# Level exponents of gated linear attention: from one running sum by subtraction on DVE, in place of eight mask products on TensorE

## The chip, the core and the metric

The kernel runs on one core of a Trainium2 chip. The metric is the device time of one execution in microseconds (us); lower is better. Instructions run on TensorE (PE; its weight loads are listed as PEld), VectorE (DVE), ScalarE (ACT) and GpSimd (POOL). SyncE (SP) issues DMA transfers and does no arithmetic. Each engine executes its own list of instructions in a fixed order. Where an instruction needs what another engine has not yet made, it waits, and everything behind it on its engine waits with it.

## The reference, cut to what matters

The program is two layers of one kind (`hybrid_layer`) followed by one layer of another kind. All arithmetic is in fp32 on 256 tokens of width 1024. Each of the first two layers has three branches: sparse attention (NSA), gated linear attention (GLA) and attention to a memory. They are gated, merged and followed by an MLP. The change touches GLA alone:

```python
log_a = jax.nn.log_sigmoid((g_low @ w_gate + b_gate)) / GLA_TAU       # tau = 16; (256, 4 heads x 64)
def step(state, xs):                                                  # one chunk of the sequence
    b = jnp.cumsum(ab, axis=2)
    decay = jnp.exp(jnp.where(tril, b[:, :, :, None, :] - b[:, :, None, :, :], -jnp.inf))
    attn = jnp.einsum('bhid,bhjd,bhijd->bhij', qb, kb, decay)
    o = attn @ vb + jnp.einsum('bhid,bhdv->bhiv', qb * jnp.exp(b), state)
    ...
```

The result does not depend on the size of a chunk, and the kernel does not use the reference's 64. It works on two tiles of 128 tokens.

## The kernel before, in words

**The weight stream.** Most of PE's time goes to products of activations with fp32 weight matrices. A weight unit of 128x1024 is fetched by DMA into a `raw` tile (four of them). It is then split into two halves: `hi` by ACT (L431; every sixth one by POOL, L429), and `lo = raw - hi` by DVE (L432). There are four `hi` and four `lo` tiles. A product is then three matmuls of 512 columns: `hi,hh`, `lo,hh` and `hi,hl`, where `hh` and `hl` are the halves of the activations. Three such matmuls are called a group below. PE needs `hi` and `lo` of a unit before the group that uses them, so DVE stands in the path of the weight stream.

**What stands between the groups.** The attention work consists of small matmuls that depend on ACT, DVE and POOL work between them. It is written as Python generators: `gla`, `nsa_att`, `nsa_cmp` and `mem_chain`. The order of PE's instructions is fixed by hand. Each matmul advances a planned clock by an estimate (`pe_time`, L175). Between two groups the function `pump` (L138) lets every generator go on whose due time has passed. A generator gives its next due time by `yield n`, in planned nanoseconds. Every matmul that a generator emits then stands in PE's list at that place. The order on DVE, ACT, POOL and SP is made by a scheduler from the whole program and is fixed as well.

**GLA (`gla`, L984).** `T` is the log-sigmoid of the gate, two tiles of 128 tokens by 256 columns, split in halves `Th` and `Tl`. For a tile the kernel needs sums of `T` over ranges of tokens. The ranges come from a tree: level 1 splits 128 tokens in two halves of 64, level 2 splits each into 32, down to level 7 with single tokens. For a token in the upper half of its block the range goes from the middle of the block to the token. For one in the lower half it goes from behind the token to the middle. There are also level 0 (from behind the token to the tile's end, for the first tile) and level 8 (from the tile's start to the token, for the second tile). Each tile uses eight levels.

Before, these sums are matmuls. `MLR` is a constant of nine 0/1 matrices of 128x128, side by side. For each tile and each pair of heads, two halves of four levels (512 columns) are formed, each by two matmuls (`Th` and `Tl`) into one PSUM tile `pd` (L1009 to L1014), with a `yield 600.0` behind each half. ACT reads `pd` and writes `exp(pd/16)` to `E`, the tile `b8x` in the profile (L1014, four times per tile). Then `E` is multiplied by the keys: L1018 gives `KE`, L1026 levels 1 to 7 (odd levels on DVE, even ones on POOL), L1020 is level 8 by the queries. After `yield 5350.0`, `q_side` (L1032, L1041) writes the query side of a level to one of four `QB` tiles. For each level PE multiplies `QB` with `E` (L1050), DVE copies the valid part into the score tile `A` (copy_predicated, L1054), and the next `q_side` follows.

**Around it.** While the first tile goes through this, DVE also serves NSA's softmax: reductions of the scores to their maxima (L892, L913), reciprocals, scaling of `pexp` (L902, L922), copies of `pts` (L936). While the second tile goes through it, DVE serves the NSA compression chain: `KB` (L832), which PE multiplies in 32 small matmuls, then the chain on `n` and `cd` behind it (L848 to L864), and the branch gates (L1129). The mask constant is loaded once in the program by `const_l` (two DMAs through `mraw` tiles, converted by POOL at L380), and its level 8 is used again at L1406, in the last layer.

## Time and profile before

| | us |
|---|---|
| median of 3 runs | 1231.71 |
| lowest, highest run | 1228.67, 1232.16 |
| the profiled execution's own time | 1227.59 |
| its span, first to last instruction | 1225.8 |
| PE busy in it | 1200.9 (98%) |
| DVE busy | 852.6 (70%) |
| ACT busy | 583.1 (48%) |
| POOL busy | 213.7 (17%) |
| mean granted TensorE clock | 0.997 |

Rows of the timeline read: start in us from the span's start, length in us, engine, line, operation, output<-inputs, shape, how many were put together (x4), and in brackets the idle time of the engine ahead of it with the engine, tile and line that ended it. Lengths on PE overlap, since matmuls are pipelined: the distance between two starts is what one costs, not the length. The same holds, by less, on DVE, where the next instruction often starts before the end of the one ahead of it. Rows of the groups give count, then minimum, median and maximum of a duration in ns, then the first and last start. A row of a table of windows gives the window, its length, and the busy time (and number) of PE, PEld, DVE, ACT and POOL in it, then the granted TensorE clock, the DMA share and GB/s.

### The profile page before, as it was taken

What the parts mean: (1) busy time and instruction counts of PE and PEld (TensorE: products, weight loads), DVE (VectorE), ACT (ScalarE), POOL (GpSimd) and SP (SyncE); (2) the same over time, 40 slices, a digit from 0 to 9 for tenths busy, and PEclk for the clock granted to TensorE, in tenths of its full rate; (3) what the DMA queues carried; (4) which work ended last, traced back from release to release, by engine and by line L of the source; (5) the groups of instructions that cost most, each with busy time, mean ns of one, the idle gap of its engine ahead of it and who ended that gap; (6) DMA issues with size and microseconds to landing.
All of it is one profiled execution on the core that took longest, in us unless ns stands there. A gap on an engine that the chain in (4) does not pass through costs nothing. (4 is left out here: it accounts for less than half of the span.)

```text
span 1225.8 us, 18640 instructions
## 1 busy us (share of the span) xinstructions
PE 1200.9 (98%) x7069; PEld 1028.4 (84%) x7069; DVE 852.6 (70%) x1389; ACT 583.1 (48%) x926; POOL 213.7 (17%) x236
## 2 busy tenths in 40 slices
PE   8999999999999999999999999999999999999997
PEld 5787677888899899888777888999988997998876
DVE  5867988667654545668878767654554799985676
ACT  6566644444644434456655334543443334443351
POOL 2210220120111212210221030121121111000202
PEclk9999999999999999999999999999999999999998
DMA  8566523786656665656723676566566555466561
GB/s 296 179 174 179 170 87 108 220 224 213 200 188 185 190 190 177 188 160 164 202 66 114 198 209 200 167 193 194 183 189 195 178 178 164 139 186 192 172 207 67
DMA packets 139469, 217.10 MB, mean 177 GB/s; under 512 B 12145, under 2 KB 77013, under 8 KB 139380
## 3 DMA queue, kind: packets, MB, share of 16 engines
q1 hardware_dynamic: 137460, 209.47, 57.0%
q0 software_dynamic: 1920, 6.46, 1.8%
q8 instruction: 55, 0.90, 0.3%
q14 instruction: 34, 0.28, 0.1%
HBM read 215.01 MB, written 1.05 MB: 176 GB/s over the span
## 5 line engine op out<-in xcount | busy, mean ns | idle before, releaser
L432 DVE TENSOR_TENSOR lo<-raw,hi 128x1024 fp32r<-128x1024 f32 (+1 forms) x369 | 462.2, 1257 | 259.3 <-ACT hi L431 213.1
L431 ACT ACTIVATE hi<-raw 128x1024 fp32r<-128x1024 f32 (+1 forms) x308 | 324.6, 1058 | 428.2 <-PE acc L188 284.0
L188 PE MATMUL acc<-hi,hh 128*128 128x512 f32 (+1 forms) x512 | 205.7, 402 | 0.0
L188 PE MATMUL acc<-hi,hl 128*128 128x512 f32 (+1 forms) x512 | 197.1, 385 | 0.0
L188 PE MATMUL acc<-lo,hh 128*128 128x512 f32 (+1 forms) x512 | 196.7, 384 | 0.0
L429 POOL TENSOR_SCALAR hi<-raw 128x1024 fp32r<-128x1024 f32 x61 | 78.0, 1278 | 613.8 <-PE acc L188 476.5
L188 PE MATMUL acc<-hi,oh 128*128 128x512 f32 x400 | 157.9, 395 | 0.0
L188 PE MATMUL acc<-lo,oh 128*128 128x512 f32 x400 | 155.9, 390 | 0.0
L188 PE MATMUL acc<-hi,ol 128*128 128x512 f32 x400 | 155.9, 390 | 0.0
L188 PE MATMUL psm<-hh,hi 128*128 128x256 f32 x448 | 126.8, 283 | 0.0
L188 PE MATMUL psm<-hh,lo 128*128 128x256 f32 x448 | 126.8, 283 | 0.0
L188 PE MATMUL psm<-hl,hi 128*128 128x256 f32 x448 | 126.8, 283 | 0.0
L188 PEld LDWEIGHTS acc<-hi,hh 128*128 128x128 f32 x512 | 96.4, 188 | 20.4 <-issue 4.0
L188 PEld LDWEIGHTS acc<-hi,hl 128*128 128x128 f32 x512 | 96.1, 188 | 19.4
L188 PE MATMUL acc<-hh,hi 128*128 128x256 f32 x384 | 111.8, 291 | 0.0
L188 PEld LDWEIGHTS acc<-lo,hh 128*128 128x128 f32 x512 | 96.5, 188 | 16.3
L188 PE MATMUL acc<-hh,lo 128*128 128x256 f32 x384 | 108.7, 283 | 0.2 <-DVE lo L432 0.2
L188 PE MATMUL acc<-hi,b8x 128*128 128x512 f32 (+1 forms) x336 | 105.4, 386 | 3.6 <-ACT hi L444 2.1
L188 PE MATMUL acc<-hl,hi 128*128 128x256 f32 x384 | 108.8, 283 | 0.0
L188 PEld LDWEIGHTS acc<-hi,ol 128*128 128x128 f32 x400 | 75.1, 188 | 15.8
L188 PEld LDWEIGHTS acc<-hi,oh 128*128 128x128 f32 x400 | 75.2, 188 | 14.8
L188 PEld LDWEIGHTS acc<-lo,oh 128*128 128x128 f32 x400 | 75.2, 188 | 14.5
(362 smaller groups left out, 1869.5 us busy)
## 6 DMA issues: line engine op xcount, KB each, us to landing
raw<-in_w_in SPq DMA_DIRECT2D x160, 512.0 KB
raw<-in_w_up SPq DMA_DIRECT2D x64, 512.0 KB
raw<-in_w_down SPq DMA_DIRECT2D x64, 512.0 KB
raw<-in_w_branch SPq DMA_DIRECT2D x28, 512.0 KB
raw<-in_w_out SPq DMA_DIRECT2D x24, 512.0 KB
raw<-in_cmp_w SPq DMA_DIRECT2D x32, 256.0 KB
raw<-in_mem_w_kv SPq DMA_DIRECT2D x15, 512.0 KB
gate<-in_b_merge POOLq DMA_DIRECT2D x6, 1024.0 KB, 7.6
```

The lines of the kernel that those rows point to most:

```text
L188: nc.tensor.matmul(o, l, r, start=start, stop=stop, skip_group_check=True)
L429: pool.tensor_scalar(hi, raw, 1.0, 1.0, op0=OP.mult, op1=OP.mult)
L431: act(hi, raw, AF.Copy)
L432: dve.tensor_tensor(lo, raw, f32(hi), op=OP.subtract)
```

## The change

`MLR` becomes one 128x128 matrix (t <= i). Eight matmuls of 128 columns, for both tiles at once and into one PSUM tile, give the running sum of `T` over the tokens of a tile. Two ACT copies bring it to SBUF, to the new constants' tiles `CUM`. For each level DVE then forms the exponent by two subtractions of 128x128 elements each: the running sum minus its value at the middle for the upper halves, the reverse for the lower ones. Level 0 is one subtraction of 128x256, and level 8 is the running sum itself. That is 15 subtractions in the first tile and 14 in the second. ACT's Exp works over four levels of both head pairs (1024 elements) in place, so there are two per tile. In the second tile the last one is split, 768 elements from `E` and 256 from `CUM`. The yields of 600 are replaced by one `yield 3000.0`.

In the program's lists: PE has 6336 rows in place of 6352, DVE 1287 in place of 1229 (29 more in each of the two layers), ACT 753 in place of 754, POOL 210 in place of 213, SP 440 in place of 441. `const_l` is 64 KB in place of 576 KB. Lines of the kernel after the change are other ones: L425 is `lo` (L432 before), L1012, L1018 and L1019 are the subtractions, L1038 the key products (L1026), L1053 `q_side` (L1041), L1066 the copy of scores (L1054).

```diff
-    ml[0] = t > i
-    ml[8] = t <= i
+    ml = (t <= i).astype(np.float32)
...
-    MLR = consts.tile([P, 9 * 128], FR, name="MLR")
+    MLR = consts.tile([P, 128], FR, name="MLR")
+    CUM = [consts.tile([P, 2, 128], F32, name=f"CUM{i}") for i in range(2)]
...
-        for c0, c1 in ((0, 1024), (1024, 1152)):
-            mraw = wraw.tile([P, 1024], F32, tag="raw", name=nm("mraw"))
-            nc.sync.dma_start(mraw[:, 0:c1 - c0], const_l[:, c0:c1])
-            pool.tensor_scalar(MLR[:, c0:c1], mraw[:, 0:c1 - c0], 1.0, 1.0, op0=OP.mult, op1=OP.mult)
+        nc.sync.dma_start(mraw[:, MASK_W:MASK_W + P], const_l)
+        pool.tensor_scalar(MLR, mraw[:, MASK_W:MASK_W + P], 1.0, 1.0, op0=OP.mult, op1=OP.mult)
...
+        pd = PS()
+        for tt in range(2):
+            for pr in range(2):
+                o = pd[:, 256 * tt + pr * P:256 * tt + pr * P + P]
+                mm(o, Th[:, tt, pr * P:pr * P + P], MLR, True, False)
+                mm(o, Tl[:, tt, pr * P:pr * P + P], MLR, False, True)
+        for tt in range(2):
+            act(CUM[tt].rearrange("p a b -> p (a b)"), pd[:, 256 * tt:256 * tt + 256], AF.Copy)
         for tt in range(2):
             ts_ = slice(tt * P, tt * P + P)
+            C = CUM[tt]
             E = B8("b8x", shape=(2, 8, 128))
-            for pr in range(2):
-                for hf in range(2):
-                    pd = PS()
-                    rhs = MLR[:, 128 * tt + 512 * hf:128 * tt + 512 * hf + 512]
-                    mm(pd, Th[:, tt, pr * P:pr * P + P], rhs, True, False)
-                    mm(pd, Tl[:, tt, pr * P:pr * P + P], rhs, False, True)
-                    yield 600.0
-                    act(E[:, pr, 4 * hf:4 * hf + 4, :].rearrange("p a b -> p (a b)"), pd, AF.Exp, scale=1.0 / 16)
+            for l2 in range(8):
+                idx = l2 if tt == 0 else l2 + 1
+                if idx == 0:
+                    dve.tensor_tensor(E[:, :, l2, :], C[:, :, 127:128].to_broadcast([P, 2, 128]), C, op=OP.subtract)
+                elif idx < 8:
+                    s = 64 >> (idx - 1)
+                    e = E[:, :, l2, :].rearrange("p a (n u s) -> p a n u s", u=2, s=s)
+                    c = C.rearrange("p a (n u s) -> p a n u s", u=2, s=s)
+                    m = c[:, :, :, 0, s - 1:s].to_broadcast([P, 2, 64 // s, s])
+                    dve.tensor_tensor(e[:, :, :, 1, :], c[:, :, :, 1, :], m, op=OP.subtract)
+                    dve.tensor_tensor(e[:, :, :, 0, :], m, c[:, :, :, 0, :], op=OP.subtract)
+                if l2 % 4 == 3:
+                    last = idx == 8
+                    es = E[:, :, l2 - 3:l2 + (0 if last else 1), :]
+                    act(es, es, AF.Exp, scale=1.0 / 16)
+                    if last:
+                        act(E[:, :, l2, :], C, AF.Exp, scale=1.0 / 16)
+            yield 3000.0
```

**Places in the order.** The first is DVE in layer 0 while the first tile's exponents are formed. `pexp` are the probabilities of NSA's softmax, `lo` the low halves of the weight stream, `b8x` is `E`. Before:

```order
L902 TENSOR_SCALAR pexp_1358<-pexp_1358,r_250_1364 128x128 x4
L913 TENSOR_REDUCE n_261_1405<-psm_1401 128x2
L919 RECIPROCAL r_258_1389<-s_257_1386 128x2
L920 TENSOR_TENSOR r_258_1389<-r_258_1389,GT_548 128x2
L922 TENSOR_SCALAR pexp_1385<-pexp_1385,r_258_1389 128x256 x2
L919 RECIPROCAL r_264_1411<-s_263_1408 128x2
L920 TENSOR_TENSOR r_264_1411<-r_264_1411,GT_548 128x2
L922 TENSOR_SCALAR pexp_1407<-pexp_1407,r_264_1411 128x256 x2
L432 TENSOR_TENSOR lo_1446<-raw_1444,hi_1445 128x1024
```

And now, from the last two of the first twelve subtractions on (ten more stand ahead of these rows, and one, L1012, ahead of the `pexp` at L895 that answers to L902):

```order
L1018 TENSOR_TENSOR b8x_1381<-CUM_120 128x2x32x2
L1019 TENSOR_TENSOR b8x_1381<-CUM_120 128x2x32x2
L906 TENSOR_REDUCE n_253_1406<-psm_1402 128x2
L425 TENSOR_TENSOR lo_1446<-raw_1444,hi_1445 128x1024
L1018 TENSOR_TENSOR b8x_1381<-CUM_120 128x2x64
L1019 TENSOR_TENSOR b8x_1381<-CUM_120 128x2x64
L912 RECIPROCAL r_256_1412<-s_255_1409 128x2
L425 TENSOR_TENSOR lo_1452<-raw_1450,hi_1451 128x1024
L913 TENSOR_TENSOR r_256_1412<-r_256_1412,GT_550 128x2
L906 TENSOR_REDUCE n_274_1463<-psm_1459 128x2
L915 TENSOR_SCALAR pexp_1408<-pexp_1408,r_256_1412 128x256 x2
```

The subtractions stand ahead of the softmax's two further reductions (L906) and of its scalings (L915), and two `lo` have come in ahead of the second reduction. The second further scaling, `pexp_1465`, and the first `QB` stand nine rows further down, behind products with the keys.

The second place is DVE in layer 0 around `KB`, the tile that PE needs for the 32 small matmuls of the compression chain. Before:

```order
L832 TENSOR_SCALAR KB_1771<-psm_1769,COL 128x32
L432 TENSOR_TENSOR lo_1954<-raw_1952,hi_1953 128x1024
L936 COPY pts_1794<-psm_1790 128x384
L892 TENSOR_REDUCE n_362_1803<-psm_1796 128x4
L848 TENSOR_TENSOR n_367_1835<-psm_1818,CF 128x128 x2
```

And now, from the last four of the twelve subtractions that stand right behind `KB` (L825):

```order
L1018 TENSOR_TENSOR b8x_1783<-CUM_121 128x2x16x4
L1019 TENSOR_TENSOR b8x_1783<-CUM_121 128x2x16x4
L1018 TENSOR_TENSOR b8x_1783<-CUM_121 128x2x32x2
L1019 TENSOR_TENSOR b8x_1783<-CUM_121 128x2x32x2
L929 COPY pts_1824<-psm_1820 128x384
L885 TENSOR_REDUCE n_356_1833<-psm_1826 128x4
L1018 TENSOR_TENSOR b8x_1783<-CUM_121 128x2x64
L1019 TENSOR_TENSOR b8x_1783<-CUM_121 128x2x64
L841 TENSOR_TENSOR n_361_1865<-psm_1848,CF 128x128 x2
```

The `lo` that stood behind `KB` has left this place, and the second tile's subtractions stand there.

The third place is where that `lo` and its followers stand now, DVE behind the compression chain. `gate` is a branch gate, `a_364` the score tile `A`:

```order
L855 TENSOR_TENSOR cd_1874<-cd_1874,GT_550 128x16
L1141 SCALAR_TENSOR_TENSOR gate_1716<-acc_1718,xrs_506,gate_1716 128x512
L857 TENSOR_TENSOR n_361_1865<-n_361_1865,cd_1874 128x256
L1066 COPY_PREDICATED a_364_1913<-MASKS,psm_1923 128x4x64
L1053 TENSOR_TENSOR QB_124<-b8x_1783,a_168_938 64x2x64 x2
L1141 SCALAR_TENSOR_TENSOR gate_1716<-acc_1719,xrs_506,gate_1716 128x512
L425 TENSOR_TENSOR lo_1941<-raw_1939,hi_1940 128x1024
L425 TENSOR_TENSOR lo_1947<-raw_1945,hi_1946 128x1024
L425 TENSOR_TENSOR lo_1953<-raw_1951,hi_1952 128x1024
L425 TENSOR_TENSOR lo_1959<-raw_1957,hi_1958 128x1024
L1066 COPY_PREDICATED a_364_1913<-MASKS,psm_1971 128x8x32
```

PE's list at that place, from the first `QB` product of the second tile on:

```order
L182 MATMUL psm_1923<-QB_124,b8x_1783 128x128 x2
L182 MATMUL acc_1719<-hi_1739,hh_132 128x512
L182 MATMUL acc_1719<-lo_1740,hh_132 128x512
L182 MATMUL acc_1719<-hi_1739,hl_133 128x512
L182 MATMUL acc_1937<-hi_1940,hh_132 128x512
L182 MATMUL acc_1937<-lo_1941,hh_132 128x512
```

The second matmul of the group on `acc_1937` needs `lo_1941`. That tile is made on DVE behind the gate and the copy of scores, and three more `lo` stand between it and the next copy of scores.

More of the change, by code (lines that the diff above doesn't have):

```diff
@@ L50, in shape_constants @@
     cf[:, CO_IDENT:CO_IDENT + 128] = np.eye(128)
-    ml = np.zeros((9, 128, 128), np.float32)
     lm = np.zeros((128, MASK_W), np.float32)
@@ L59, in shape_constants @@
         s = b // 2
-        mid = (i // b) * b + s
-        up = (i % b) >= s
-        ml[l] = np.where(up, (t >= mid) & (t <= i), (t > i) & (t < mid))
         low = ((t // b) == (i // b)) & ((t % b) < s) & ((i % b) >= s)
@@ L80, in shape_constants @@
     dm[:, 256:384] = dm[:, 0:128]
-    ml = ml.transpose(1, 0, 2).reshape(128, -1).copy()
     return cf, cb, lm, ml, dm
@@ L1405, in layer_2 @@
             tr(pt[:, g * P:g * P + P], sgw[:, g], IDF)
-        dve.tensor_tensor(WMT, v4(pt), f32(MLR[:, None, 8 * P:9 * P]).to_broadcast([P, 4, 128]), op=OP.mult)
+        dve.tensor_tensor(WMT, v4(pt), f32(MLR[:, None, :]).to_broadcast([P, 4, 128]), op=OP.mult)
         SGB = A2([P, 4, 128])
```

## The prediction

> **What bounds the kernel now.** I read the page's busy times first, then windows around the two places in the program where GLA forms its exponents, then the timelines of PE and DVE there.
>
> ```profile
> span 1225.8 us, 18640 instructions
> PE 1200.9 (98%) x7069; PEld 1028.4 (84%) x7069; DVE 852.6 (70%) x1389; ACT 583.1 (48%) x926; POOL 213.7 (17%) x236
> ```
>
> PE is the bound: 24.9 us of the span are not PE's. So work taken from PE is worth its full time, as long as no other engine makes PE wait in its place. The mean of 70% for DVE says nothing about the stage that changes. For that I cut layer 0 and layer 1 at the same three points: the first tile's exponents to the end of its scores, then the second tile's up to its first scores, then the rest.
>
> ```profile
> 120.50:153.50 33.00, 31.49 (x193) 23.20 (x193) 29.88 (x70) 21.44 (x60) 8.67 (x14) 1.00 0.59 178
> 153.50:174.60 21.10, 21.10 (x127) 16.72 (x127) 15.82 (x42) 8.63 (x19) 6.41 (x10) 1.00 0.22 63
> 174.60:198.40 23.80, 22.95 (x150) 18.34 (x148) 19.85 (x45) 13.04 (x34) 2.23 (x3) 1.00 0.40 123
> 591.00:624.30 33.30, 31.94 (x197) 23.57 (x195) 29.41 (x70) 20.55 (x59) 8.95 (x14) 1.00 0.58 175
> 624.30:645.00 20.70, 19.91 (x119) 15.69 (x119) 14.57 (x41) 9.16 (x21) 7.61 (x10) 1.00 0.22 60
> 645.00:669.30 24.30, 23.04 (x148) 18.41 (x148) 20.32 (x45) 11.71 (x33) 3.81 (x4) 1.00 0.40 123
> ```
>
> The fourth number of a row is DVE. In the first stretch DVE is busy 29.88 of 33.00 us, while PE waits 1.5. DVE is the second bound there, with 3.1 us to spare. The two layers agree within a microsecond, so I work out layer 0 and double it.
>
> **What PE gives up.** Sixteen mask matmuls of 512 columns per layer, in eight pairs.
>
> ```profile
> L188 PE MATMUL psm<-MLR,T x32: 389/398/499, 120.5 to 637.6; 128*128 128x512 f32 x32
> 120.49 0.72 PE L188 MATMUL psm<-MLR,T 128*128 128x512 f32 x2
> 121.04 0.40 PE L188 MATMUL acc<-hi,hh 128*128 128x512 f32 x1
> 126.47 0.39 PE L188 MATMUL acc<-hi,hh 128*128 128x512 f32 x1
> 127.16 0.39 PE L188 MATMUL acc<-hi,hh 128*128 128x512 f32 x1
> 92.75 0.28 PE L188 MATMUL acc<-hh,hi 128*128 128x256 f32 x1
> 92.86 0.28 PE L188 MATMUL acc<-hl,hi 128*128 128x256 f32 x1
> ```
>
> From one start to the next a pair costs 0.55 us (120.49 to 121.04); 8 pairs are 4.4 us. No matmul of 128 columns of this number type stands in the trace. The nearest row has 256 columns and costs 0.11 to 0.12 from start to start; half of it, 0.06, is the low bound and its length alone, 0.28, the high one. I take 0.12, since such a short product may cost as much as the next longer: 8 x 0.12 = 1.0 (0.5 to 2.2). PE gives up 3.4 us per layer, 6.8 in all (4.4 to 7.8). A group of three costs 0.69 (126.47 to 127.16), a figure needed below.
>
> **What DVE takes on.** 29 subtractions per layer.
>
> ```profile
> L1026 DVE TENSOR_TENSOR b8x<-b8x,a x16: 276/281/587, 130.6 to 640.3; 128x128 f32<-128x128 f32 x16
> 169.39 0.48 DVE L1026 TENSOR_TENSOR b8x<-b8x,a 128x128 f32<-128x128 f32 x2
> 169.79 0.41 DVE L1020 TENSOR_TENSOR b8x<-b8x,a 128x256 f32<-128x256 f32 x1
> 130.57 1.41 DVE L1026 TENSOR_TENSOR b8x<-b8x,a 128x128 f32<-128x128 f32 x4
> ```
>
> These are products of the same size on the same strided views. One takes 0.28 us, but two in a row take 0.40 to the next start (169.39 to 169.79), 0.20 each. Beside POOL work four take 1.41, 0.35 each. I take 0.205: the subtractions stand in rows of twelve, and POOL has nothing to do until they are done. The 256-wide one has 0.41. First tile 14 x 0.205 + 0.4 = 3.3 us, second 14 x 0.205 = 2.9; per layer 6.2 (0.28 each gives 8.2). [...]
>
> ACT's Exp goes over the same elements in fewer instructions, plus two copies; ACT is at 21.44 of 33.00, and I cost it at nothing. If its cover were gone, the two copies would add about two lengths of the 256-wide Exp, under 1.1 us. The smaller `const_l` saves one DMA and one conversion by POOL (17% busy) and I cost it at nothing too; below, nothing excludes a gain of a few tenths.
>
> **First tile.** The order shows the subtractions ahead of the softmax's scalings and of the first `QB`.
>
> ```profile
> 126.73 0.17 DVE L919 RECIPROCAL r<-s 128x2 f32<-128x2 f32 x1 [0.67 <-ACT pexp L917]
> 132.37 1.85 DVE L1041 TENSOR_TENSOR QB<-b8x,a 64x128 f32<-64x128 f32 x4
> 133.55 0.68 PE L188 MATMUL psm<-QB,b8x 128*128 128x128 f32 x4
> 143.43 0.68 PE L188 MATMUL psm<-QB,b8x 128*128 128x128 f32 x4 [0.46 <-DVE tmp L791]
> 145.57 0.71 PE L188 MATMUL psm<-QB,b8x 128*128 128x128 f32 x4 [0.18 <-DVE a L1054]
> 152.76 0.55 PE L192 MATMUL psm<-CF,pexp 128*128 128x128 f32 x3 [0.86 <-DVE a L1054]
> ```
>
> Everything else ahead of the first `QB` is the same work (two `lo`, the reductions, the scalings). So DVE comes to it later by 3.3 less the idle 0.67 that it had there: 2.65 us. The first `QB` product starts at 136.2 instead of 133.55. PE would be there 1.2 us earlier (4 x 0.55 - 8 x 0.12, all eight narrow ones standing in this stretch), at 132.35, and waits 3.85 us. Later in this tile, PE's own waits on DVE of before, 0.46 + 0.18 + 0.86 = 1.5 us, and the remaining idle time of DVE take most of the lag back: DVE's work in the stretch becomes 29.88 + 3.3 = 33.2, and of its idle time only the 0.7 at the start can't be filled, so the stretch takes some 33.2 to 33.9 instead of 33.0. I take **+0.6 us** (between -1.2, all hidden, and +2.65, none taken back).
>
> **Second tile.** Here the subtractions stand behind `KB`, in time that DVE spent waiting for PE's `KB` product. They are free themselves, but they push out the `lo` that was made there (155.57 below).
>
> ```profile
> 155.57 1.23 DVE L432 TENSOR_TENSOR lo<-raw,hi 128x1024 fp32r<-128x1024 f32 x1
> 162.33 0.71 PE L188 MATMUL psm<-MLR,T 128*128 128x512 f32 x2
> 162.52 0.49 DVE L848 TENSOR_TENSOR n<-psm,CF 128x128 f32<-128x128 f32 x2 [2.79 <-PE psm L188]
> 163.66 0.87 PE L188 MATMUL pso<-pts,n 128*64 128x256 f32 x8
> 164.47 0.72 PE L188 MATMUL psm<-MLR,T 128*128 128x512 f32 x2
> 170.71 2.62 DVE L432 TENSOR_TENSOR lo<-raw,hi 128x1024 fp32r<-128x1024 f32 x2
> 173.85 0.74 DVE L1129 SCALAR_TENSOR_TENSOR gate<-acc,xrs,gate 128x512 f32<-128x512 f32 x1
> 174.51 0.68 DVE L913 TENSOR_REDUCE n<-psm 128x2 f32<-128x512 f32 x1
> 175.11 0.43 DVE L1054 COPY_PREDICATED a<-MASKS,psm 128x256 f32<-128x256 uint8 x1
> 176.03 0.75 DVE L1129 SCALAR_TENSOR_TENSOR gate<-acc,xrs,gate 128x512 f32<-128x512 f32 x1
> 175.69 0.68 PE L188 MATMUL psm<-QB,b8x 128*128 128x128 f32 x4 [0.35 <-DVE a L1054]
> 180.06 0.68 PE L188 MATMUL psm<-QB,b8x 128*128 128x128 f32 x4 [0.50 <-DVE a L1054]
> 651.92 0.68 PE L188 MATMUL psm<-QB,b8x 128*128 128x128 f32 x4 [1.26 <-DVE a L1054]
> ```
>
> Count from T, the end of the `KB` product (162.33). DVE goes on 0.19 later, does the chain on `n` and the first `QB` in 8.2 (162.52 to 170.71), then two gates at 0.66 (173.85 to 174.51), a copy of scores and two `QB` (0.92 together, 175.11 to 176.03), and `lo` in 1.23: ready at T + 11.8. PE has eight groups (5.5), the `pso` products (0.81, 163.66 to 164.47), one `QB` product (0.4) and a matmul of 0.23 ahead of it, and meanwhile waits about 0.5 for that `QB`: it arrives at T + 7.4 and **waits 4.4 us** for `lo`. The three `lo` behind it (3 x 1.2) hold the next copy of scores. I expect a wait near the 1.26 of layer 1 there, in place of the 0.35 + 0.50 of before: +0.4. Against this, PE gives up four pairs here, 2.2 us. Sum: 0.5 + 4.4 + 0.4 - 2.2 = +3.1 us, if nothing is taken back. In the third stretch DVE is idle 4 of 23.8 us, and in the second it waits 2.79 for `KB`. Both can give some of it back; all of it would end at -2.2. I take **+1.4**, a little on the side of the full wait.
>
> **Sum.** 0.6 + 1.4 = +2.0 per layer, +4 us for both. Against the profiled execution's 1227.59 (1.8 more than its span) that is 1231.6. The median of the runs stands 4.1 higher than that execution, so for the median it is 1231.71 + 4.0 = **1235.7 us**.
>
> **Rivals.**
>
> *DVE has room, PE keeps its saving.* If the lag is taken back in both tiles, the full 6.8 stays: 1224.9; if half of it does, 1228.3. For it: DVE is idle 30% of the whole, and the second tile's subtractions fall into a wait. Against it: 3.3 us more on an engine that has 3.1 to spare in the first stretch. It is on the other side, and it decides from the point where the two waits (3.85 and 4.4) leave less than 3.4 us per layer at the end of the third stretch.
>
> *Wait and saving cancel.* The waits of tile two are half of mine, as the 2.79 idle ahead of the chain on `n` lets DVE start it with nothing queued, and PE loses about what it gives up: 1231.7.
>
> *The granted clock drops in the new waits.* A wait of some 4 us could make the clock fall for a while.
>
> ```profile
> 33.13 0.63 PE L192 MATMUL psm<-CF,X 128*128 128x128 f32 x4 [2.92 <-DVE kss L579]
> 33.00:37.00 4.00, 3.87 (x19) 3.32 (x20) 3.63 (x12) 2.23 (x6) 0.00 (x0) 1.00 0.05 2
> ```
>
> After a wait of 2.92 us the granted clock (the number behind POOL's) is 1.00 in the next 4 us. The waits that I expect are longer. If the clock halved for as long as such a wait, about 4 us, each would cost 2 us more: with one or two per layer 1239.7 to 1243.7. [...]
>
> *The subtractions cost 0.28 each.* Then DVE has 1.1 us more in the first tile and PE waits for it, and in the second they still fit the wait for `KB`: +1.1 per layer, 1237.9. A narrow matmul at 0.28 would take 1.2 per layer from the saving, but they stand ahead of the wait and are hidden in it.
>
> **How the numbers follow.** A difference of 0.3% (3.7 us) is about what a measurement can tell from none. Chances: the forecast with its waits not taken back 0.44 (1233 to 1238.5), cancelling 0.28 (1229 to 1233), the saving kept 0.17 (1224 to 1229), dearer subtractions 0.06, the clock 0.05. The likeliest case's own range is 1233 to 1238.5. The range 1227 to 1241 leaves out the full saving and the clock's drop twice per layer, together under 2 in 10. Slower by over 0.3% (above 1235.4): half of the forecast's case and most of the last two, with the part of cancelling that drifts up: 0.44. Faster (below 1228.0): most of the saving kept, and a little of cancelling: 0.17. The rest, 0.39, is within.
>
> **What would show it.** Right: a PE wait of 3 to 4.5 us ahead of the first `QB` product of the first tile, and another of about 4 on `lo` (L425) some 7 us behind the `KB` product, in both layers; `psm<-MLR,T` eight per layer at about 0.12 from start to start; subtractions at about 0.2 in a row. The three stretches, cut at the same points, would be longer in the second and third and nearly equal in the first. Wrong: the first stretch shorter by a microsecond, or no wait of over 2 us behind `KB`. Then DVE's list was not the limit, or PE came later to it than I counted, and the time falls below 1229. A granted clock under 0.9 behind a wait would show the clock's rival.

## The result, and the profile after

The kernel after takes 1249.39 us (median of 4 executions, 1242.16 to 1251.46) against 1231.93 us before (4 executions): a ratio of 1.0137, with a 95% interval from 1.011 to 1.0164. A second comparison with the same two kernels (the last repeat below) gave 1.0113 (1.008 to 1.0147). By the medians the change makes the kernel slower by 17.5 us here and by 13.1 us in the second comparison. The forecast was 1235.7 us, with a range up to 1241.

The head of the page, with a span of 1240.4 us against 1225.8 before:

```profile
span 1240.4 us, 18659 instructions
PE 1206.3 (97%) x7053; PEld 1030.6 (83%) x7053; DVE 859.8 (69%) x1447; ACT 584.6 (47%) x924; POOL 214.0 (17%) x235
```

Over the two layers PE has 16 narrow matmuls in place of 32 wide ones, and still it is busy 5.4 us longer. That is the first sign that its instructions themselves took longer. Next, both kernels are cut into windows at the same three matmuls in each layer: the first product with `MLR`, the first `KB` product, and the first group on `oh` behind GLA. The kernel before:

```profile
120.49:158.84 38.35, 36.84 (x226) 27.08 (x226) 33.57 (x79) 23.60 (x63) 8.67 (x14) 1.00 0.57 172
158.84:198.37 39.53, 38.69 (x242) 31.16 (x241) 31.94 (x77) 19.49 (x50) 8.64 (x12) 1.00 0.29 90
591.40:630.51 39.11, 36.96 (x226) 27.10 (x225) 33.04 (x79) 22.91 (x62) 9.86 (x15) 1.00 0.54 165
630.51:670.25 39.74, 38.48 (x242) 31.17 (x241) 32.22 (x77) 19.42 (x50) 10.51 (x12) 1.00 0.30 90
```

The kernel after, at the same matmuls:

```profile
122.55:166.02 43.47, 38.58 (x230) 28.30 (x229) 38.03 (x105) 24.93 (x65) 11.45 (x15) 0.96 0.49 148
166.02:206.86 40.84, 37.09 (x228) 29.61 (x226) 32.06 (x77) 18.02 (x45) 7.66 (x11) 0.96 0.29 90
601.26:644.46 43.20, 38.40 (x231) 28.31 (x229) 37.27 (x105) 24.36 (x64) 11.58 (x16) 0.96 0.48 146
644.46:684.79 40.33, 37.08 (x228) 29.64 (x226) 31.34 (x77) 18.13 (x45) 7.51 (x11) 0.96 0.29 92
```

The first tile (first and third row) is longer by 5.1 and 4.1 us, the second one by 1.3 and 0.6: 11.1 us of the 14.6 between the two spans. (PE's list differs by more than the `MLR` products: two groups of three matmuls, 1.4 us, that stood behind the first `KB` product stand ahead of it now. On equal work the first tile is longer by 3.7 and 2.7 us and the second by 2.7 and 2.0.) PE's idle time in these four windows (length less PE's busy time) was 5.8 us and is 16.7. And the granted clock, 1.00 in all four before, is 0.96 in all four after.

The sum for these windows: the narrow products save 7.0 us (below), new waits cost 16.7 - 5.8 = 10.9, and four stretches of halved clock of 3.4 us each cost half of that, 6.8 in all. That makes 10.7 of the 11.1 measured. The remaining 3.5 us of the span lie elsewhere, 2.1 of them ahead of GLA, where the clock was halved once more behind a wait for `kss` at 33.5 us.

PE's waits, the largest ones (sum, count, longest):

```profile
PE acc L182 <- DVE lo L425: 7.4, 4, 3.5
PE psm L186 <- DVE pexp L915: 5.8, 3, 2.7
PE psm L186 <- DVE kss L572: 2.8, 1, 2.8
PE psm L182 <- DVE QB L1053: 2.8, 2, 1.7
```

Their places on PE's timeline in layer 0:

```profile
122.55 1.09 PE L182 MATMUL psm<-MLR,T 128*128 128x128 f32 x8
123.47 0.45 PE L182 MATMUL acc<-hi,hh 128*128 128x512 f32 x1
...
137.11 0.44 PE L186 MATMUL psm<-CF,pexp 128*128 128x128 f32 x2 [2.67 <-DVE pexp L915]
139.26 1.16 PE L182 MATMUL psm<-QB,b8x 128*128 128x128 f32 x4 [1.71 <-DVE QB L1053]
140.07 0.77 PE L182 MATMUL acc<-hi,hh 128*128 128x512 f32 x1
140.64 0.63 PE L182 MATMUL acc<-lo,hh 128*128 128x512 f32 x1
141.07 0.63 PE L182 MATMUL acc<-hi,hl 128*128 128x512 f32 x1
...
181.95 0.50 PE L182 MATMUL acc<-lo,hh 128*128 128x512 f32 x1 [3.49 <-DVE lo L425]
```

Behind the two waits of the first tile a matmul of 512 columns lasts 0.63 us and the next starts 0.43 us later, where it was 0.39 and 0.23. The windows of the kernel after around its waits and around the `KB` product show the clock behind POOL's entry:

```profile
135.00:139.30 4.30, 0.48 (x3) 0.27 (x3) 4.25 (x12) 0.87 (x1) 2.90 (x5) 1.00 0.41 142
139.30:142.70 3.40, 3.40 (x10) 2.57 (x10) 3.29 (x7) 0.00 (x0) 1.07 (x1) 0.50 0.21 35
166.00:170.00 4.00, 4.00 (x36) 3.96 (x35) 1.93 (x6) 3.01 (x10) 2.98 (x7) 1.00 0.00 0
170.00:173.40 3.40, 3.40 (x13) 1.88 (x13) 3.40 (x17) 0.42 (x1) 0.27 (x1) 0.50 0.00 0
178.40:182.00 3.60, 0.11 (x2) 0.05 (x1) 3.56 (x7) 0.78 (x2) 1.14 (x1) 1.00 0.00 0
182.00:190.00 8.00, 7.74 (x43) 6.24 (x44) 7.70 (x13) 3.17 (x8) 2.49 (x2) 1.00 0.74 244
```

The clock is halved behind the first tile's waits (139.3) and behind the `KB` product (170.0), but not behind the longest single wait, the 3.49 us for `lo`.

Why `lo` is late shows on DVE's timeline of the kernel after:

```profile
177.13 0.75 DVE L1141 SCALAR_TENSOR_TENSOR gate<-acc,xrs,gate 128x512 f32<-128x512 f32 x1 [1.85 <-PE acc L182]
...
178.56 0.43 DVE L1066 COPY_PREDICATED a<-MASKS,psm 128x256 f32<-128x256 uint8 x1
...
180.01 0.75 DVE L1141 SCALAR_TENSOR_TENSOR gate<-acc,xrs,gate 128x512 f32<-128x512 f32 x1
180.68 4.94 DVE L425 TENSOR_TENSOR lo<-raw,hi 128x1024 fp32r<-128x1024 f32 x4
```

DVE itself stood idle 1.85 us at the head of its list, waiting for PE's group on `acc`, while four `lo` stood behind the two gates. PE then waited for the first of these. That is a chain from PE to DVE and back, given by the order of the list. DVE was busy all through PE's wait (3.56 of 3.60 us), but just ahead of that wait it had idled for 1.85 us, longer than one `lo` takes (4.94 us for four).

### The profile page after: what moved, and what is told of

The parts are those of the page before. It is cut to its first block, busy times and chain, and to the rows that moved or that the text cites. A ratio compares the mean times of both kernels' runs of the same rounds, so it can differ in the third digit from the quotient of the medians.

```text
span 1240.4 us, 18659 instructions
## 1 busy us (share of the span) xinstructions
PE 1206.3 (97%) x7053; PEld 1030.6 (83%) x7053; DVE 859.8 (69%) x1447; ACT 584.6 (47%) x924; POOL 214.0 (17%) x235
## 5 line engine op out<-in xcount | busy, mean ns | idle before, releaser
L425 DVE TENSOR_TENSOR lo<-raw,hi 128x1024 fp32r<-128x1024 f32 (+1 forms) x369 | 460.9, 1253 | 265.4 <-ACT hi L424 216.9
L182 PEld LDWEIGHTS acc<-hi,ol 128*128 128x128 f32 x400 | 75.1, 188 | 15.9
L182 PEld LDWEIGHTS acc<-lo,oh 128*128 128x128 f32 x400 | 75.2, 188 | 14.6
```

Source lines behind the costliest of these rows:

```text
L182: nc.tensor.matmul(o, l, r, start=start, stop=stop, skip_group_check=True)
L425: dve.tensor_tensor(lo, raw, f32(hi), op=OP.subtract)
```

## The experiments

The runs that change something follow below in the order of the question that they answer. "Clock" is the mean granted clock of an execution. "Lost" is (1 - clock) times its time: half of the time that it spent at half clock.

### Repeats of both kernels: how time follows the clock

> The kernel before, unchanged, to see the granted clock of its other executions. The profile before had a clock of 0.997 at 1227.59 us, while three timed executions of the kernel after had 0.981 to 0.983 at 1248.5 to 1251.5 us and its profile 0.991 at 1242.16. If the halved clock belongs to the new waits alone, every execution of the kernel before stays at 0.995 or more and within 1227 to 1233 us. If stretches of halved clock come and go in this program whatever the kernel, some executions fall below 0.993, and time rises by about 0.6 us for each 0.0005 lost.

Measured: 1229.46 us (10 executions, clock 0.992 to 0.997), ratio to the other executions of the kernel before 0.9982 (0.9964 to 1.0). Together with the executions that stood beside the other runs there are 100 of the kernel before, on four chips: a median of 1230.9 us at a clock of 0.994. Their time depends on the clock:

| clock | executions | median us |
|---|---|---|
| 0.997 | 9 | 1229.4 |
| 0.996 | 20 | 1228.9 |
| 0.994 | 12 | 1230.7 |
| 0.993 | 14 | 1232.8 |
| 0.992 | 11 | 1233.7 |
| 0.991 | 11 | 1235.2 |
| 0.990 | 3 | 1236.4 |

A line through all 100 rises by 0.91 us for each us lost (correlation 0.90). So the kernel before has halved stretches too, about two per execution besides the one at its end (7.4 us lost in the middle one, 3.3 in the profile with the end alone, 1.7 for each). The profile that the prediction was read from happened to have none. In this repeat's profile there is one right behind the `KB` product:

```profile
157.00:160.30 3.30, 3.30 (x33) 3.30 (x31) 0.70 (x2) 1.51 (x8) 0.00 (x0) 1.00 0.30 114
160.30:163.70 3.40, 3.40 (x12) 2.27 (x13) 2.56 (x11) 0.90 (x2) 0.00 (x0) 0.50 0.00 0
```

PE is busy for all 3.30 us of the first row, with small products of 16 columns, and the clock is halved behind it all the same. In the first profile of the kernel before, the same product (158.84 to 162.33) was followed by a clock of 1.00.

> The kernel after, unchanged, for more executions and a second trace at another position of the clock's steps. If the loss is waits of fixed length plus halved stretches whose number changes from one execution to the next: the waits of the first trace come again within 0.3 us (2.67 and 1.71, 3.49), the number of halved stretches is another, and over the executions time rises by 0.7 to 1.0 us for each us that the clock lost. If the waits themselves vary: they differ by more than 1 us.

Measured: 1243.51 us (4 executions, clock 0.982 to 0.991). The waits came again: 2.67, 1.74 and 3.49 us. Three of all eight executions of the kernel after have a clock of 0.991 and 1241.2 to 1242.2 us, the other five 0.981 to 0.988 and 1245.4 to 1251.5. At 0.991 the kernel before has 1235.2. So at equal clock the kernel after loses 6.4 us. The rest of the difference of the medians (1246.3 of eight against 1230.9 of 100, 15.4) goes with the clock, some 9 us. The expected rise of time with the clock did not quite come: over these eight it is 0.6 us for each us lost, where 0.7 to 1.0 was expected, and an execution at 0.982 (1245.44 us) was faster than one at 0.988 (1247.17). A lost us is thus not always worth the same in this kernel, and by this slope the clock's part is nearer 7 us.

### PE kept at work in the waits

```diff
+    def fill(o, n):       # products of a bf16 constant, results unused
+        ...
                 tr(pt[:, 0:P], E0[pr][:, 2 * j + w], IDF)
+                if pr == 0 and w == 0 and j == 1:
+                    fill(pt[:, P:512], 14)
...
+                if lev == 1 and tt == 0:
+                    fill(pa[:, 0:512], 6)      # ahead of the first QB product
...
+                if k == 0 and FILL[0]:         # first group behind tile 1's first QB product
+                    fill(ps[tt], 13)
```

> The kernel after with TensorE kept at work where it waited: per layer 14 products of 384 columns and 6 of 512 (bf16 constants, results unused) ahead of the last softmax transposes and the first QB product, 13 of 512 ahead of the group that waits for lo. DVE's list is unchanged, so each late tile is ready at the same time and the filled time was idle before. If the halved clock behind the waits is the larger part of the loss (three timed executions of the kernel after had a clock of 0.981 to 0.983, some 22 us lost, against 6 of the kernel before at 0.995): the clock comes back to 0.990 or more, 1233 to 1238 us. If the waits alone are the loss: no gain, 1249 or some 2 us more where a filling is longer than its wait.

Measured: 1239.40 us (1238.06 to 1241.74), ratio 1.0063 (1.0037 to 1.0088), clock 0.991 to 0.994 in all five executions. The windows of this run at the times where the kernel after waited and was halved:

```profile
135.00:139.30 4.30, 3.91 (x24) 2.27 (x23) 4.19 (x13) 0.90 (x1) 2.97 (x5) 1.00 0.40 138
139.30:142.70 3.40, 3.40 (x24) 2.04 (x24) 3.39 (x5) 0.60 (x1) 2.21 (x3) 1.00 0.32 64
```

More work on PE made the kernel faster: the softmax's last tile and `lo` are as late as before, but the clock stays at 1.00. (DVE's list did not stay quite unchanged: in layer 0 a copy of `pts` moved behind the first `QB`, and the `QB` product came 0.6 us sooner; in layer 1 it came 0.1 us later.) Of the loss against the kernel before some 7 to 10 us come back (against 1246.3 or 1249.4 us; 6 to 9 by the ratios), as the clock's theory says. The two halved stretches behind the `KB` products remain (167.4 and 645.3 us in its profile), as nothing was filled there. What is left, 1239.4 against 1232.8 at the same clock of 0.993, is again 6.6 us. In the profile of the kernel after, new waits less PE's saving make 3.9 us in GLA's windows (10.9 - 7.0); where the rest lies is not shown.

### The `KB` product in two halves

```diff
                 mm(pcv[:, tt, 16 * h:16 * h + 16], QS[:, h, tt * P:tt * P + P], KB[:, h % 2, :], True, True)
+            if tt == 0:
+                yield 200.0
```

This is the kernel before with one pause.

> The kernel before with a pause of 200 planned ns in the middle of the 32 small products of KB, so that one group of three full products stands between the two halves; nothing is left out. In the executions looked at, the clock was halved for 3.4 us right behind the KB products (160 to 168 and 635 to 648 us) in most kernels, the one before among them. If the small products, which use 16 columns at a time for 3.5 us, are what the clock reacts to, the halved stretches there are gone: clock 0.996 to 0.997, 2 to 3 us faster, about 1228, less what a changed DVE list may take. If not, the clock stays at 0.995.

Measured: 1240.27 us (1235.69 to 1243.76), 1.0066 (1.0046 to 1.0086), clock 0.988 to 0.994. In the profile the stretch behind the two halves is at full clock, and the halved one comes behind two new waits (1.55 and 2.36 us):

```profile
161.60:167.10 5.50, 5.50 (x46) 4.69 (x45) 1.05 (x4) 2.10 (x9) 0.00 (x0) 1.00 0.17 66
167.10:170.50 3.40, 3.40 (x17) 2.85 (x17) 3.08 (x11) 2.22 (x4) 1.78 (x4) 1.00 0.00 0
174.00:177.50 3.50, 1.63 (x8) 0.88 (x6) 3.50 (x7) 0.17 (x1) 1.73 (x1) 1.00 0.47 133
177.50:184.30 6.80, 4.75 (x16) 4.13 (x16) 3.66 (x8) 1.78 (x4) 0.73 (x1) 0.50 0.41 133
```

So the mechanism came out as expected in this profile, and the gain did not: one pause of 200 planned ns reordered DVE's list behind `KB` and made waits of its own. As a way to a faster kernel it failed.

That a halved stretch behind `KB` comes and goes without any change has a reason that the traces of all 19 profiled runs show. Within each execution the halved stretches start whole multiples of 3.413 us apart, so it can be cut into steps of that length. The clock of a step goes by what PE did in the step ahead of it:

| a step at full clock, in which | steps | followed by a halved one |
|---|---|---|
| 22 to 32 of the 32 small products of `KB` stand | 29 | 29 |
| 16 to 21 of them stand | 12 | 4 |
| 1 to 15 of them stand | 23 | 0 |
| none stands, PE busy under 40% | 43 | 43 |
| none stands, PE busy 40 to 60% | 61 | 14 |
| none stands, PE busy over 60% | 6588 | 0 |

Of 36 `KB` products in one piece, 33 were followed by a halved stretch. The three that were not had at most 21 of their small products in one step, and both of those of the first profile of the kernel before are among them (21 and 16). The two products split here have 16 in each step, and neither was followed by one. So the clock was halved behind the small products by themselves, when a step held enough of them (22 or more in every case, 16 to 21 in 4 of 12).

The wait of 3.49 us for `lo` falls into two steps of the kernel after, and PE is busy for about half of each:

```profile
176.84:180.26 3.42, 1.62 (x10) 1.06 (x8) 3.08 (x6) 0.63 (x1) 1.92 (x2) 1.00 0.00 0
180.26:183.67 3.41, 1.72 (x11) 1.50 (x12) 3.41 (x4) 1.01 (x2) 0.24 (x1) 1.00 0.04 9
```

The two waits of the first tile fall into one (135.88 to 139.30), in which PE is busy for 0.48 us.

### The subtractions taken out, whole or by tile

```diff
-                if idx == 0:
+                if SKIP:          # True, tt == 1 or tt == 0
+                    pass
+                elif idx == 0:
...
-                    act(es, es, AF.Exp, scale=1.0 / 16)
+                    act(es, C[:, :, None, :].to_broadcast([P, 2, n, 128]), AF.Exp, scale=1.0 / 16)   # where skipped
```

> The kernel after without any subtraction: Exp reads the running sum itself for every level, so the level exponents are left out. PE's narrow products, the copies and ACT's work stay. Theory 1 (the subtractions' place in DVE's list makes PE wait): without them PE keeps the 3.4 us per layer, about 1225 us, clock as before. Theory 2 (the narrow products, the yield of 3000 or the new order of PE make the loss): it stays near the kernel after, 1240 or more.

> The kernel after with the first tile's 15 subtractions only; the second tile's exponents are left out (Exp reads the running sum), and DVE's list behind the compression chain's KB is that of the run without subtractions. Theory 1: two waits ahead of the first QB product in each layer, 4.4 us together (2.67 and 1.71 in the profile after), each layer one halved stretch of 3.4 us behind them: 8.8 + 3.4 us over the run without subtractions, about 1237. If DVE takes the lag back, under 1229.

> The kernel after with the second tile's 14 subtractions only; the first tile's exponents are left out. DVE's list behind KB is that of the kernel after: lo of the next gate unit stands behind two gates. Theory 1: one wait of about 3.5 us on that lo in each layer and little else, 7 us over the run without subtractions, and up to 3.4 more where the clock is halved behind the KB product: 1232 to 1236. If the second tile's subtractions are hidden as they fall into DVE's wait for KB, under 1227.

Measured: without subtractions 1233.37 us, 1.0026 (1.0004 to 1.0048); with the first tile's alone 1240.16, 1.0054 (1.0034 to 1.0074); with the second's alone 1241.82, 1.0065 (1.004 to 1.0091). (The ratios stand against executions of the kernel before from the same times on the same chip, with a median of 1231.34; a ratio is not that of the medians shown.) Each tile's subtractions bring the waits that the kernel after has at that tile, to 0.03 us: 2.67 and 1.74 with the first tile's (and 2.96 for `n`, see below), 3.49 with the second's. So the waits are theirs. My numbers for the two were 3 and 6 us too low. For the second tile's alone the clock was 0.988 in three of four executions, and waits for `g` and `a` (2.7 and 2.5 us) stood beside those for `lo`; with the first tile's alone there were waits for `n` (5.2 us in both layers).

The run without subtractions missed 1225 by 8 us, and this was the larger surprise. PE had its saving and no subtraction stood anywhere, and yet the kernel was no faster. PE and DVE of that run:

```profile
176.14 0.41 PE L186 MATMUL psm<-CF,n 128*128 128x128 f32 x2 [2.97 <-DVE n L857]
```

```profile
166.34 0.87 DVE L895 TENSOR_SCALAR pexp<-pexp,r 128x128 f32<-128x128 f32 x4
170.44 1.23 DVE L425 TENSOR_TENSOR lo<-raw,hi 128x1024 fp32r<-128x1024 f32 x1 [3.23 <-ACT hi L424]
171.58 0.49 DVE L849 TENSOR_TENSOR n<-n,CF 128x128 f32<-128x128 f32 x2
```

DVE's list had been made anew, and a `lo` whose `hi` was not there yet stood ahead of the compression chain's `n`. DVE idled 3.23 us with `n` behind it, and PE then waited 2.97 us for `n`.

### That wait moved

```diff
-        yield 7050.0
+        yield 10500.0      # ahead of the transposes of n
```

> The run without subtractions (the level exponents are left out, Exp reads the running sum) with one pause changed: 10500 planned ns in place of 7050 ahead of the transposes of the compression chain's n, so that they stand some 3.4 us later in PE's list; DVE's list is the same up to n. In the run without subtractions PE waited 2.97 and 2.2 us there, while DVE stood 3.2 us at the head of its list with a lo whose hi was not there. If PE's saving was lost to that wait alone: it is gone, about 1228 us. If other work takes the place of the wait (the scores behind it are late then, or the next chain), 1231 or more.

Measured: 1229.02 us, 0.9983 (0.9962 to 1.0004), clock 0.992 to 0.997. The wait for `n` is gone, and 4.4 us came with it. So a good part of PE's saving had been spent on that wait. Even so the run without any subtraction is only about 2 us below the kernel before, not 7, and the interval does not exclude no difference at all.

### The same work at other places

The next four runs keep all the subtractions on DVE and change only pauses:

```diff
-        yield 8600.0                  # ahead of the running sum
+        yield 5000.0                  # early sum; 6500.0 and 5500.0 in the last two
...
-            yield 5350.0              # ahead of the first QB product
+            yield 8500.0              # early sum with late QB; 7000.0 in the last two
```

> The kernel after with the pause ahead of the running sum at 5000 planned ns instead of 8600, so that the sums stand earlier in PE's list and the first tile's subtractions ahead of NSA's score reductions in DVE's, where DVE was idle 3.2 of 4 us (112 to 116 us in the profile after); in the second tile lo is no longer behind two gates in a row. If the place of the subtractions makes the waits: no wait over 2 us in either tile, clock at 0.993 or more, 1226 to 1233. If their amount does: waits of the same sum at other places, over 1240.

> The kernel after, with all 29 subtractions per layer on DVE, but two pauses changed: 5000 planned ns ahead of the running sum (8600) and 8500 ahead of the first QB product (5350), since with the early sum alone PE came to QB 3.9 us too soon. If the loss is a matter of where the products stand in PE's list against DVE's: waits of less than 2 us, clock 0.993 or more, 1227 to 1233. If the amount of DVE work sets it: 1238 or more, with the waits at other places.

> The kernel after with 6500 planned ns ahead of the running sum and 7000 ahead of the first QB product (5000 and 8500 in the run that came level with the kernel before). The sum stands where T is ready, which took 0.9 us per layer there; twelve of the second tile's subtractions stand ahead of KB in DVE's list. If the amount is harmless wherever the lists agree: PE's saving shows for the first time, 1226 to 1230 at a clock of 0.994. If the level result was the best that the amount allows: 1232 or more.

> As that run with 5500 ahead of the sum: the first tile's subtractions stand ahead of all of the first layer's NSA reductions, and the second tile's twelve ahead of KB with one lo beside the chain on n. Expected where order decides: within 3 us of the run with 6500, 1226 to 1231. If small shifts of the lists move the time by several us by themselves: anything from 1226 to 1245.

Measured: the early sum alone 1245.43 us, 1.0112 (1.0081 to 1.0142). With a late `QB` as well **1233.60 us, 1.0012 (0.9994 to 1.0029)**. The pairs 6500/7000 and 5500/7000 gave 1241.61, 1.0101 (1.0084 to 1.0118), and 1242.17, 1.0107 (1.0092 to 1.0122).

The early sum put the subtractions into DVE's idle time, but PE then came to `QB` too soon:

```profile
133.37 0.68 PE L182 MATMUL psm<-QB,b8x 128*128 128x128 f32 x4 [3.92 <-DVE QB L1053]
```

With the second pause changed too, the same product waits 0.43 us, and the largest waits of that run in GLA's windows are these:

```profile
PE psm L182 <- DVE a L1066: 3.4, 3, 1.3
...
PE psm L182 <- DVE T L515: 1.8, 2, 0.9
PE psm L182 <- DVE pts L929: 1.6, 2, 0.9
```

So all 29 subtractions per layer can stand on DVE without making the kernel slower than before, and their amount alone does not fix the loss. It may still cost something: the run without any and with a late `n` has a ratio lower by 0.0029, 3.6 us, with other lists. And the outcome depends on the pauses: both runs that should have been better still are 8 to 9 us slower than the one that came level, with waits on `QB` (6.2 and 4.4 us), `n` and `ck` that I had not foreseen. None of them shows PE's saving.

The subtractions in pieces:

```diff
+                if l2 % 2 == 1:
+                    yield 600.0
                 if l2 % 4 == 3:
...
-            yield 3000.0
+            yield 600.0
```

> The kernel after with its subtractions in pieces: a pause of 600 planned ns behind every two levels, as the kernel before had four per tile, and 600 in place of 3000 behind them. In DVE's list one of the two reductions and one scaling of the softmax move ahead of part of the first tile's subtractions; the twelve behind KB stay, but lo stands behind the chain on n and two gates as one of three. If order is what counts, the first tile's waits shrink to 2 to 3 us and the second's to 2, and time is 1236 to 1243; if pieces don't matter, 1247 to 1252.

Measured: 1238.73 us, 1.0063 (1.0042 to 1.0084), clock 0.987 to 0.992: the time is as the theory of the order said. The waits are not quite. The first tile's are 0.65 and 1.03 us, with 1.29 more for `pts`; the second tile's is 2.50, for `QB`.

### The amount of work on DVE changed

The kernel before with the subtractions added as dead work (E is overwritten by Exp; PE's list is unchanged):

```diff
             E = B8("b8x", shape=(2, 8, 128))
+            C = f32(Th[:, tt]).rearrange("p (a b) -> p a b", a=2)
+            for l2 in range(8):
+                ...      # the same subtractions, from C into E
             for pr in range(2):
```

> The kernel before, with its mask products and PE's list as they are, and the same 29 subtractions per layer added on DVE, written to E ahead of Exp, which overwrites them (dead work). DVE's list has the first tile's ahead of NSA's score reductions, the second tile's behind KB as in the kernel after, but one lo stands soon behind the KB product's chain begins. If the amount of DVE work makes the waits: 3.3 us per layer in the first tile at least, and halved clock behind them, 1240 or more. If it is only where the work stands relative to lo and the softmax: 1231 to 1236.

Measured: 1238.43 us, 1.0046 (1.0023 to 1.0069), clock 0.989 to 0.996: between the two expectations, so this one decides little. No wait in GLA's windows is longer than 1.51 us. It shows that the wide mask products are no protection: the same DVE work costs there too, some 6 us with PE's list as it was.

Levels 2, 4 and 6 on POOL, first in the kernel after, then with the early sum and late `QB`, then with late `n` as well:

```diff
-                    dve.tensor_tensor(e[:, :, :, 1, :], c[:, :, :, 1, :], m, op=OP.subtract)
-                    dve.tensor_tensor(e[:, :, :, 0, :], m, c[:, :, :, 0, :], op=OP.subtract)
+                    eng = dve if idx % 2 else pool
+                    eng.tensor_tensor(e[:, :, :, 1, :], c[:, :, :, 1, :], m, op=OP.subtract)
+                    eng.tensor_tensor(e[:, :, :, 0, :], m, c[:, :, :, 0, :], op=OP.subtract)
```

> The kernel after with the subtractions of levels 2, 4 and 6 on POOL instead of DVE: 12 of 29 per layer leave DVE, 2.5 us. In DVE's list the lo behind KB comes back to its place near KB, and 8 instead of 14 subtractions stand ahead of the softmax. POOL's cost by its products of the same size, 0.5 us each, 6 us per layer, 3 in each tile, beside DVE. If order is what costs: the wait on lo is gone and the first tile's two waits fall from 4.4 to some 3 us: 1235 to 1240 with a clock of 0.990. If POOL's slower instructions set the end of Exp instead, the waits stay and time is 1245 or more.

> As the run with an early sum and a late QB, with the subtractions of levels 2, 4 and 6 on POOL (17 of 29 left on DVE). If the amount on DVE still counts beside the order: 2 us or more faster than that run. If only the order counts: the same within 1.5 us. PE's saving of 3.4 us per layer would show as 1224 to 1228.

> As the run with levels 2, 4 and 6 on POOL, and the transposes of the compression chain's n 3.4 us later in PE's list (10500 for 7050 planned ns), which took 4.4 us off the run without subtractions. If n's chain is again what PE waits for: 2 to 5 us faster than the run beside it, 1223 to 1228. If not, the same or slower as the scores behind n come later.

Measured: 1236.31 us, 1.004 (1.0019 to 1.0062); 1245.96, 1.0102 (1.0064 to 1.014); 1245.06, 1.0106 (1.0079 to 1.0133). In the first the wait on `lo` is gone and the two of the first tile are 2.09 and 0.82 us, as expected. The other two contradict what I expected: with less DVE work than the run that came level they are 12 us slower, with waits for `ck`, `g` and `r`; the late `n` changed nothing beside the run ahead of it. Less work on DVE at these places did not help, and these runs do not separate the amount from the order, since the list came out differently. No version was found that beats the kernel before.

## Why the prediction was wrong

The direction was right and the size was not: +4.0 forecast, +17.5 measured in the first comparison and +13.1 in the second. By the steps:

- **What PE gives up** was right. The eight narrow products take 0.92 us together (122.55 to 123.47), 0.115 each, against 0.12 forecast, so PE gives up 3.5 us per layer.
- **What DVE takes on** was right. In the kernel after, twelve subtractions in a row start 0.20 us apart:

```profile
126.51 0.29 DVE L1018 TENSOR_TENSOR b8x<-CUM 128x128 f32<-128x128 f32 x1
126.71 0.29 DVE L1019 TENSOR_TENSOR b8x<-CUM 128x128 f32<-128x128 f32 x1
```

  One lasts 0.27 to 0.29 us where twelve stand in a row, in both tiles, and the next starts 0.20 us after it. So a row costs the distance that the forecast took, not the length (0.28 each would have made 8.2 us per layer).
- **First tile**: the wait was forecast at 3.85 us ahead of `QB` and measured as 2.67 + 1.71 = 4.38, split by the softmax's last transposes. The step that failed is the next one, "and the remaining idle time of DVE take most of the lag back", which took the tile to +0.6. The prediction's own first stretch, cut at the same matmuls, takes 37.27 us where it was 33.00 (with one group of matmuls more and six transposes fewer):

```profile
122.55:159.82 37.27, 32.38 (x191) 23.54 (x190) 31.96 (x87) 20.77 (x59) 11.45 (x15) 0.95 0.53 158
```

  DVE is busy for 31.96 us of it, so it had 5.3 us idle, and the lag stayed all the same. PE's wait was not given back by idle time on DVE further on: PE's list went on from where it stood, and what it had lost could come back only where PE had waited later anyway. Before's own waits there were 1.5 us, and that is all there was to take back. Up to the `KB` product, idle time adds 3.4 us to the tile, the halved clock 1.7 and the two groups that moved 1.4, and the `MLR` products take 1.8 off: 4.7 of the 5.1 measured in layer 0.
- **Second tile**: the wait for `lo` was forecast at 4.4 us and measured as 3.49 and 2.98. The tile was forecast at +1.4 and measured at +1.3 and +0.6, but that agreement is luck: a halved stretch behind `KB` (+1.7) and the two groups that left (-1.4) are in the measured number and not in the forecast. From the start of the `KB` product (166.02) to the group with `lo` (181.95) it is 15.9 us, where T + 11.8 makes 15.3; PE came there later than I counted, since the halved clock behind `KB` held it up as well, and so waited less. The order rows had told where `lo` would be late and by about how much.
- **The granted clock** is where most of the miss is. I gave this rival 0.05 and priced it rightly per stretch (2 us; half of 3.4 is 1.7). Its number came out too (one or two per layer; two in the profile of the kernel after), but partly by luck, since one of the two stands behind the `KB` product and not behind a new wait. Its time for two per layer, 1243.7 us, is that of the second comparison (1243.5); the first lies 6 us above it. What I had wrong is the condition. I asked whether one wait of some 4 us makes the clock fall, for an estimated 4 us, and held the 2.92 us at 33.13 against it. But a step that held two waits with 0.4 us of work between them was followed by a halved one (135.88 to 139.30), and so were steps full of the small `KB` products, with no wait at all, while a wait of 3.49 us that two steps shared went without a halved stretch. Every halved stretch in the traces, but for the one at the end of each execution, is 3.4 us long or twice that, and those of one execution start whole multiples of 3.41 us apart (33.48, 139.30, 170.02, 617.16 and 647.88 us in the kernel after: 31, 9, 131 and 9 steps). What counts is how much of one such step PE spends with little to do (the table above), and that depends on where the steps happen to lie. I had argued against a fall of the clock from a single wait in a single profile.
- **From the profiled execution to the median** I added the same 4 us to both. The timed executions of the kernel after lost more clock (0.981 to 0.983 in the first three) than its profiled one (0.991), so 7 us of the first median lie in that step. The profile before was also one of the luckier ones: at 1227.59 us it had no halved stretch but that at its end.

Of the rivals, the saving kept and the two that cancel did not happen. The run that came level with two other pauses shows that the second was possible with the same work. The dearer subtractions did not happen either (0.20 us each). What stays open is why PE's 7 us come out in none of the runs: the two that come closest still wait on `T`, `a`, `pts` or `g`, and no run had all of these moved.

## What to carry to other kernels

Where an engine at 98% gives up work and the others follow lists fixed in advance, the saving can turn into waits: here 7.0 us of it stood against 10.9 us of new idle time on PE. Ask which tile becomes late next, and price its wait in full, since idle time on another engine may not pay it back (DVE's 5.3 us in the first tile did not). Then look at what a wait does to TensorE's clock. In these traces it was halved for 3.41 us behind each full-clock step of that length in which PE was busy under 40% (43 of 43), and behind each that held 22 or more products of 16 columns (29 of 29). So sum up what PE does in any 3.4 us around a wait, count such small products as little, and keep PE at work where nothing else can be moved (the filled waits gave back 7 to 10 us). And compare more than one execution of each kernel by clock, since one profile can be a lucky one. Last, a list made by a scheduler moves as a whole: taking work out or adding one pause put other tiles late here, so read the new list before the time.

## What was not expected of the hardware

- The clock was halved behind 3.3 us in which PE was busy without a gap, with products of 16 columns (the repeat of the kernel before, 157.0 to 160.3 us); so it was behind all 29 steps of 3.41 us that held 22 or more of them.
- Steps without them were followed by a halved one in 43 of 43 cases where PE was busy under 40% of the step, and in 14 of 61 between 40 and 60%.
- Unused products made the kernel after 7 to 10 us faster, with the clock at 0.991 to 0.994 where it was 0.981 to 0.991.
- 100 executions of the kernel before, on four chips, spread over 1226.4 to 1237.6 us, most of it with the clock: time follows it at 0.91 us for each us lost (correlation 0.90).
- Subtractions of fp32 with runs as short as one element (level 7) start 0.20 us apart in the first tile, like those with runs of 64. In the second tile the two of level 7 stand 0.43 us apart, while POOL works beside them.
